# Combining weights of dilated attention broadcast one dilation at a time on GpSimd's queue, the next pair's q and k loaded earlier

## The chip, the cores and the metric

The kernel runs on one core of a Trainium2 chip. The core has five engines with a queue of instructions each: TensorE (PE, matrix products; PEld is its weight load), VectorE (DVE), ScalarE (ACT), GpSimd (POOL) and SyncE (SP, which only issues DMAs here). Each engine works through its own instructions in order; DMAs can be issued by SyncE, ScalarE and GpSimd. The metric is the device time of one execution in microseconds (us).

## The reference, cut to what matters

One decoder layer on 2048 positions of 1024 features. The input is projected; one branch is a Mamba-2 scan (chunked, with a convolution and a gate), the other is causal attention of 16 heads of 64 in a dilated window, computed for three dilations and then combined:

```python
o1, l1 = dilated_window_attention(q, k, v, slopes, 1)
o2, l2 = dilated_window_attention(q, k, v, slopes, 4)
o3, l3 = dilated_window_attention(q, k, v, slopes, 16)
wts = softmax(stack([l1, l2, l3]), axis=0)          # l: log of the sum of exponentials, per head and position
y_att = wts[0][..., None] * o1 + wts[1][..., None] * o2 + wts[2][..., None] * o3
y_att = rms_norm(y_att * silu(z_att), att_norm_g)
y_ssm = rms_norm(ssd(...) * silu(z_ssm), ssm_norm_g)
x = layer_norm(alpha * x + concat([y_att, y_ssm]) @ w_out, ln_g, ln_b)
```

Everything is float32. For each dilation a query sees itself and the 128 keys before it at that stride; the exponentials are not divided by their sum at once, but the sums enter the weights `wts`.

## The kernel before, in words

The kernel has three stages. The first, to about 1165 us, computes the projections, the convolution and the scan, and is not touched. It leaves in DRAM, per pair of heads, q and k (`d_q`, `d_k`, 128 x 2048), the gate (`d_za`), v in two row orders (`d_v`), and for the output projection the scan's rows (`d_us`) and the output weights (`d_wo`).

**Attention** (to about 1656 us) goes over 8 pairs of heads (`pr`). Two heads fill the 128 partitions. For each pair come the three dilations d = 0, 1, 2 (strides 16, 4, 1), for each of these four quarters `qd` of the query blocks, and for each quarter two halves: 24 steps, written (pr, d, qd, half). The step list is `todo` (L1234); the loop at L1239 writes at its turn i the scores of step i, the transposes of step i-2 and the values of step i-3. The order of the program inside this loop is what TensorE, VectorE, ScalarE and GpSimd execute (`manual_schedule`); only the order of SyncE's queue is left to the scheduler.

- `scores`: TensorE computes S = q·k for both heads. VectorE evicts it with the bias table `tb` added (L945); the same instruction leaves the row minimum of the scaled scores in a column of the statistics tile `st`. ScalarE takes the exponential and leaves the row sums in `st` (L951).
- `transposes`: TensorE transposes the exponentials, VectorE copies them to `PT`, `PC` (L968).
- `values`: TensorE multiplies with v and `vs` (v shifted by 64 rows); after the second half ScalarE copies the product N to `num[d]` (L1016 for d = 0, L1019 and L1022 for the others).
- `statistics` (L1025) transposes `st`, copies it to `sT`, and SyncE stores it to `d_st`: part 0 (d = 0 and 1) after step (1,3,1), part 1 (d = 2) after step (2,3,1), L1044.
- `gather` (L1050), right behind part 1, loads the pair's statistics back as `cm` (128 x 6 x 32: minimum and sum of three dilations, 128 x 32 positions). It is a DMA on GpSimd's queue, and waits for the stores to `d_st`.
- `weights` (L1053) makes the three combining weights per position from `cm`, nine small VectorE operations and an exponential on ScalarE, in two parts, after the values of steps (0,2,1) and (0,3,0) of the next pair. SyncE stores them to `d_wd` (L1068).
- `combine` (L1070), k = 0 to 5, all on GpSimd: k = 0, 1, 3 multiply `num[0]`, `num[1]`, `num[2]` by the weights of the dilation, which are broadcast from `d_wd` to all partitions of a tile `wb` by two DMAs of 512 KB on SyncE (L1081); k = 2 and 4 add; k = 5 multiplies by the gate, which SyncE loads into `wb` (L1096), and SyncE stores the result to `d_ua` (L1099). There are three buffers `wb` and six `num`.

Tables next to the loop hang other work behind the values of a step. `STEPS` (L1219) names for a step the part k of `combine` for the pair before, and a load: q and k of the next pair behind combine 0 and 1, at (1,0,0) and (1,1,0), v and vs for a dilation, all on GpSimd's queue (L862, L878, L880). `permute` (L904, L908) copies q into the order of a dilation on GpSimd. `LOADS` (L1222) does the same in the last pair for 1 MB tiles of `d_wo`, into buffers that attention no longer needs (`load_w`, L1116).

**The tail** (from about 1656 us) is the output projection: 16 blocks of 128 rows, each with two branches (`br` 1 is the scan, 0 attention) and two halves of the columns. `items` is the order of these products; a product (L1175 to L1177) uses a row `u` split into a rounded part on ScalarE and a rest on VectorE (`split`), fetched by `fetch_raw`; `squares` (L1143 to L1151) gives the root mean square; `add` puts the scaled product on the residual row `O`; `norm` is the layer norm. The first eight products are of the scan's rows, while pair 7 is still combined, on VectorE this time: its `weights` are written after item 1, its `combine` 0 to 2 after item 3 and 3 to 5 after item 4. The last one writes `u7` (L1092).

Of the kernel before, what the change touches and what calls it, by code (L numbers as in the profile page):

```python
# [9 lines left out]
F32 = mybir.dt.float32  # L10
# [18 lines left out]
def hybrid_layer(ctx, tc, xb, xc, w52, wv, wdt, convw, convb, dtb, alog, dskp, gcol, wout,  # L29
# [812 lines left out]
    with ExitStack() as c2:  # L842
# [137 lines left out]
        def values(A, d, qd, half, pts):  # L980
# [31 lines left out]
            if half == 1:  # L1012
                for i in range(2):
                    nm = A["N"][i][:, 0:256]
                    if d == 0:
                        nc.scalar.copy(f2(num[:, 4 * qd + 2 * i:4 * qd + 2 * i + 2, :]), nm)  # L1016
# [30 lines left out]
        def gather(A):  # L1047

            cm = A["cm"] = cm_.tile([128, 3, 2, 32], F32, name="cm")
            nc.gpsimd.dma_start(cm, dap(d_st[A["pr"]], 0, [[32, 128], [2 * S, 6], [1, 32]]))  # L1050

        def weights(A, part):

            m_, s_ = A["cm"][:, :, 0], A["cm"][:, :, 1]
            if part == 0:
# [3 lines left out]
                nc.vector.tensor_tensor(m_, mm[:, None, :].to_broadcast([128, 3, 32]), m_, op=OP.subtract)  # L1059
                nc.scalar.activation(m_, m_, AF.Exp)  # L1060
                return
            mm = A["mm"]
            nc.vector.tensor_tensor(s_, s_, m_, op=OP.mult)
# [3 lines left out]
            nc.vector.tensor_tensor(m_, m_, mm[:, None, :].to_broadcast([128, 3, 32]), op=OP.mult)
            nc.sync.dma_start(dap(d_wd[A["pr"]], 0, [[32, 128], [2 * S, 3], [1, 32]]), m_)  # L1068

        def combine(A, k):  # L1070
# [6 lines left out]
            if k in (0, 1, 3):  # L1077
                d = k - k // 2
                wb = A["wb"] = cm_.tile([128, NR, NJ], F32, name="wb", bufs=3)
                for h in range(2):  # L1080
                    nc.sync.dma_start(f2(wb[64 * h:64 * h + 64]),  # L1081
                                      dap(d_wd[pr], (d * 2 + h) * S, [[0, 64], [1, S]]))
# [11 lines left out]
            else:  # L1094
# [4 lines left out]
                nc.sync.dma_start(dap(d_ua, pr * 128, [[7 * 128, 128], [128 * 7 * 128, 16], [1, 128]]),  # L1099
# [24 lines left out]
        def fetch_raw(n, br, u=None):  # L1124
            u = raw[n, br] = (row() if u is None else u).rearrange("p (c t) -> p c t", t=128)
            queue = nc.gpsimd if (n, br) in ((3, 1), (0, 0), (1, 0)) else nc.sync
# [67 lines left out]
        def norm(n):  # L1194
# [10 lines left out]
            if n == 15:  # L1205
                for s in (slice(0, 512), slice(512, D)):
# [12 lines left out]
        STEPS = {(0, 0, 0): (None, "v", 0, 2), (0, 0, 1): (None, "vs", 0, 2), (1, 0, 0): (0, "q", 1),  # L1219
                 (1, 1, 0): (1, "k", 1), (1, 2, 0): (2, "v", 1, 0), (1, 3, 0): (3, None, 0), (2, 0, 0): (None, "v", 1, 1),  # L1220
# [8 lines left out]
        with tc.manual_schedule(engines={E.PE, E.DVE, E.Activation, E.Pool}):  # L1229
# [70 lines left out]
            for e in range(12, 16):  # L1300
                load_w(e, 1)
# [140 lines left out]
```

## Time and profile before

| | |
|---|---|
| time, median of 3 runs | 2046.55 us (2044.74 to 2047.88) |
| profiled execution: its time, its span | 2048.57 us, 2046.8 us |
| TensorE busy, weight loads | 1962.7 us (96%), 1598.1 us |
| VectorE, ScalarE, GpSimd busy | 1272.3, 1127.9, 1039.0 us |
| granted TensorE clock, mean | 0.986 |
| DMA | 447.72 MB, 219 GB/s over the span |

The rows shown below have these forms. A row of the timeline begins with the start in us and the duration; then come engine (SPq and POOLq are the DMA issues on these queues), line, operation, output<-input, the shapes, how many instructions stand together, and in brackets the idle time of the engine just before it with what ended it ("issue": nothing that the profile shows). A row of the windows has the stretch, its length, busy time and instructions of PE, PEld, DVE, ACT and POOL, the granted TensorE clock, the busy share of the DMA engines and GB/s. A row of the waits has engine, waiting operation, what it waits for, the sum in us, the number of waits, and the longest. The duration of a DMA row is that of its issue, not of its transfer. TensorE instructions are pipelined, so neighbouring rows overlap a little. Operations on GpSimd and VectorE that share a line are told apart by their tiles.

### The profile page before, as it was taken

The numbers are of one execution on the slowest core, as the hardware profiler recorded it, in microseconds if no ns is written. First come the engines' busy times: TensorE is split into PE (matmuls) and PEld (weight loads), VectorE is DVE, ScalarE is ACT, GpSimd is POOL, SyncE is SP. The second block draws the span as 40 slices with busy tenths as digits, with TensorE's granted clock in tenths as the row PEclk, the third lists the DMA queues.
The fourth block names the chain that finished last, engine by engine and source line by source line (L and its number), as shares of the span: only waits on it lengthen the run. The fifth ranks groups of instructions, "written<-read, shape, count | busy, mean of one in ns | idle before, by whom it ended". The sixth has DMA issues, their size and how long they took to land.

```text
span 2046.8 us, 42731 instructions
## 1 busy us (share of the span) xinstructions
PE 1962.7 (96%) x16024; PEld 1598.1 (78%) x16024; DVE 1272.3 (62%) x3181; ACT 1127.9 (55%) x3069; POOL 1039.0 (51%) x885
## 2 busy tenths in 40 slices
PE   7999999999999999999999999998989998999998
PEld 6788888888888888988888776666766676888886
DVE  7455464677775666644544387877777766665553
ACT  4455442466555766456566488887878851222220
POOL 3466613656655667155555424668766562432222
PEclk8999999999999999999999999999999999999999
DMA  7578695466778776987888856777787789323220
GB/s 272 164 265 288 221 331 188 133 195 194 242 252 304 252 250 252 328 264 256 277 270 268 271 179 184 215 218 236 223 235 226 217 262 314 115 97 103 87 69 31
DMA packets 232078, 447.72 MB, mean 219 GB/s; under 512 B 39520, under 2 KB 113760, under 8 KB 220864
## 3 DMA queue, kind: packets, MB, share of 16 engines
q1 hardware_dynamic: 139920, 190.02, 29.4%
q0 software_dynamic: 44000, 161.12, 23.3%
q10 hardware_dynamic: 47952, 93.87, 14.6%
q8 instruction: 126, 2.06, 0.4%
q14 instruction: 80, 0.66, 0.1%
HBM read 301.91 MB, written 151.39 MB: 221 GB/s over the span
## 4 chain that ended last, share of the span: by engine, by line
PE 81%; DMA 6%; DVE 5%; ACT 3%; issue 2%; POOL 1%; SPq 1%; ACTq 0%; POOLq 0%; DVEq 0%
PE pp L251 13%; PE pp L255 13%; PE pp L253 13%; PE N L992 5%; PE S L939 4%; PE S L1175 4%; PE S L1177 4%; PE S L1176 3%; PE pp L300 3%; PE T L966 3%; ACT P L951 2%; PE ss L300 2%; PE T L1175 2%; PE T L1176 2%; PE T L1177 2%
## 5 line engine op out<-in xcount | busy, mean ns | idle before, releaser
L208 POOL TENSOR_TENSOR w<-wr,w 128x512 fp32r<-128x512 f32 x224 | 294.0, 1324 | 225.2 <-ACT w L207 193.3
L951 ACT ACTIVATE P<-P,st 128x192 f32<-128x192 f32 (+1 forms) x768 | 322.1, 421 | 72.5 <-DVE st L945 67.7
L243 ACT COPY ev<-pp 128x512 f32<-128x512 f32 x200 | 116.5, 586 | 318.4 <-PE pp L255 283.5
L945 DVE CUSTOM_DVE_ANT_0 P<-S,tb 128x192 f32<-128x192 f32 (+1 forms) x768 | 206.5, 325 | 101.3 <-PE S L939 74.2
L263 DVE TENSOR_TENSOR ev<-pp,ev 128x512 f32<-128x512 f32 x152 | 101.2, 686 | 148.2 <-PE pp L255 100.9
L1083 POOL TENSOR_TENSOR wb<-num,wb 128x2048 f32<-128x2048 f32 x21 | 95.4, 4543 | 119.5 <-DMA wb<-d_wd 67.7
L207 ACT CAST w<-wr 128x512 fp32r<-128x512 f32 x224 | 133.6, 619 | 19.9 <-issue 7.4
L951 ACT ACTIVATION_READ_ACCUMULATOR P<-P,st 128x1 f32 x768 | 144.3, 188 | 0.0
L992 PE MATMUL N<-PT,v 128*64 128x64 f32 (+1 forms) x1536 | 125.3, 260 | 11.6 <-ACT num L1016 9.2
L968 DVE COPY PT<-T 128x512 f32<-128x512 f32 x192 | 131.7, 686 | 3.9 <-PE T L966 3.8
L966 PE MATMUL T<-ident,P 128*128 128x128 f32 x768 | 128.1, 290 | 0.3 <-DVE PT L968 0.2
L939 PE MATMUL S<-k,ex 64*64 64x192 f32 (+1 forms) x2048 | 113.0, 329 | 10.6 <-issue 10.5
L966 PEld LDWEIGHTS T<-ident,P 128*128 128x128 f32 x768 | 82.0, 142 | 47.3 <-issue 22.1
L992 PEld LDWEIGHTS N<-PT,v 128*64 128x64 f32 x1536 | 78.3, 137 | 49.2 <-issue 19.0
L202 DVE TENSOR_TENSOR wr<-wr 128x512 f32<-128x512 f32 x128 | 109.4, 854 | 8.8 <-DMA wr<-w 4.1
L454 DVE SCALAR_TENSOR_TENSOR ss<-U,cw,ss 128x512 f32<-128x512 f32 x144 | 106.0, 752 | 4.8 <-ACT ss L450 2.5
L1151 DVE TENSOR_REDUCE tb<-P 128x128 f32<-128x1024 f32 x30 | 60.0, 2000 | 44.9 <-ACT P L1148 22.5
L1213 POOL TENSOR_TENSOR k<-k,wb 128x1024 f32<-128x1024 f32 x8 | 25.8, 3225 | 120.4 <-DVE k L1212 120.4
L939 PEld LDWEIGHTS S<-k,ex 64*64 64x64 f32 x2048 | 68.1, 137 | 23.9 <-issue 17.8
L580 ACT ACTIVATE mt<-csb,cs 128x128 f32<-128x128 f32 x256 | 78.5, 392 | 1.2 <-DMA csb<-d_cs 1.2
L589 DVE TENSOR_TENSOR mt<-mt,ss 128x1024 f32<-128x1024 f32 x32 | 39.0, 1220 | 53.0 <-ACT mt L585 52.6
L251 PE MATMUL pp<-TB11h,w 128*128 128x512 f32 x176 | 69.6, 395 | 0.0
(480 smaller groups left out, 6045.0 us busy)
## 6 DMA issues: line engine op xcount, KB each, us to landing
wr<-w ACTq DMA_DIRECT2D x164, 256.0 KB
d_wc<-w SPq DMA_DIRECT2D x48, 512.0 KB
w<-d_wc POOLq DMA_DIRECT2D x48, 512.0 KB, 5.9
wb<-d_wd SPq DMA_DIRECT2D x48, 512.0 KB
d_wo<-wot POOLq DMA_DIRECT2D x32, 512.0 KB, 4.3
csb<-d_cs ACTq DMA_DIRECT2D x32, 512.0 KB
v<-d_v POOLq DMA_DIRECT2D x16, 1024.0 KB, 6.7
vs<-d_v POOLq DMA_DIRECT2D x16, 960.0 KB, 8.5
```

The lines of the kernel that those rows point to most:

```text
L207: nc.scalar.copy(h, r)
L208: nc.gpsimd.tensor_tensor(l, r, h.bitcast(F32), op=OP.subtract)
L251: nc.tensor.matmul(ps, w[:, 0, k], th[:, k], start=start and k == 0, stop=False, skip_group_check=not start)
L253: nc.tensor.matmul(ps, w[:, 0, k], tl[:, k], start=False, stop=False, skip_group_check=not start)
L255: nc.tensor.matmul(ps, w[:, 1, k], th[:, k], start=False, stop=(k == 3), skip_group_check=not start)
L939: nc.tensor.matmul(o, A["q"][d][64 * h:64 * h + 64, blk, 64 * a:64 * a + 64], kv, start=True, stop=True)
L945: nc.vector.tensor_tensor_reduce(P[:, h, cs], sp[h][:, cs], t, -0.125, 3.0e38, OP.add, OP.min, accum_out=stat(A, 0, d, h, blk))
L951: nc.scalar.activation(p, p, AF.Exp, bias=stat(A, 0, d, h, blk), scale=-1.0, accum_out=stat(A, 1, d, h, blk))
L966: nc.tensor.transpose(tp[:, h, i], P[:, h, 256 * i:256 * i + 128], ident)
L968: nc.vector.tensor_copy(pt, tp)
L992: nc.tensor.matmul(o, l, r, start=start, stop=True, skip_group_check=True)
L1175: nc.tensor.matmul(ps, uh[:, e, :], wh, start=(e == 0), stop=False)
```

## The change

The change leaves the arithmetic as it is, and moves where and when parts of it run.

- `broadcast` is a function of its own, on GpSimd's queue (SyncE's for pair 7). Dilation 0 is broadcast behind the weights at (0,3,0); the broadcast for k = 1 stands at the start of combine 0, the one for k = 3 at the start of combine 1.
- `weights` has three parts, at (0,2,0), (0,2,1) and (0,3,0). The two minima and the reciprocal stay on VectorE, the exponential on ScalarE; the subtraction, two multiplications and two additions run on GpSimd (VectorE for pair 7). The store to `d_wd` goes to GpSimd's queue (SyncE's for pair 7).
- q and k of the next pair are loaded at (0,1,0) and (0,2,0).
- Of the copies of N for d = 0 every second one runs on VectorE.
- In the last pair `gather` is on SyncE, v and vs for d = 2 are loaded at (1,0,0) and (1,0,1), the tiles of `d_wo` come at other steps, the second column halves of tiles 12 to 15 and the residual rows 0 and 1 before the end of attention.
- In the tail the weights of pair 7 are written ahead of the first item, combine 0 to 2 with the loads behind it after item 2, and 3 to 5 after item 3; residual rows 2 and 3 go to ScalarE's queue; the store of `u` of pair 6 goes to GpSimd's queue.

```diff
@@ values @@
                     if d == 0:
-                        nc.scalar.copy(f2(num[:, 4 * qd + 2 * i:4 * qd + 2 * i + 2, :]), nm)
+                        copy = nc.vector.tensor_copy if i else nc.scalar.copy
+                        copy(f2(num[:, 4 * qd + 2 * i:4 * qd + 2 * i + 2, :]), nm)
@@ gather, weights @@
-            nc.gpsimd.dma_start(cm, dap(d_st[A["pr"]], 0, [[32, 128], [2 * S, 6], [1, 32]]))
+            (nc.sync if A["pr"] == 7 else nc.gpsimd).dma_start(cm, dap(d_st[A["pr"]], 0, [[32, 128], [2 * S, 6], [1, 32]]))
...
+            last = A["pr"] == 7
+            eng = nc.vector if last else nc.gpsimd
             if part == 0:
                 mm = A["mm"] = cm_.tile([128, 32], F32, name="mm")
                 nc.vector.tensor_tensor(mm, m_[:, 0], m_[:, 1], op=OP.min)
                 nc.vector.tensor_tensor(mm, mm, m_[:, 2], op=OP.min)
-                nc.vector.tensor_tensor(m_, mm[:, None, :].to_broadcast([128, 3, 32]), m_, op=OP.subtract)
+                eng.tensor_tensor(m_, mm[:, None, :].to_broadcast([128, 3, 32]), m_, op=OP.subtract)
+            mm = A["mm"]
+            if part == 1:
                 nc.scalar.activation(m_, m_, AF.Exp)
...
+                eng.tensor_tensor(s_, s_, m_, op=OP.mult)
+                eng.tensor_tensor(mm, s_[:, 0], s_[:, 1], op=OP.add)
+                eng.tensor_tensor(mm, mm, s_[:, 2], op=OP.add)
+            if part == 2:
+                nc.vector.reciprocal(mm, mm)
+                eng.tensor_tensor(m_, m_, mm[:, None, :].to_broadcast([128, 3, 32]), op=OP.mult)
+                (nc.sync if last else nc.gpsimd).dma_start(dap(d_wd[A["pr"]], 0, [[32, 128], [2 * S, 3], [1, 32]]), m_)
+
+        def broadcast(A, k):
+            d = k - k // 2
+            wb = A["w", k] = cm_.tile([128, NR, NJ], F32, name="wb", bufs=3)
+            for h in range(2):
+                (nc.sync if A["pr"] == 7 else nc.gpsimd).dma_start(
+                    f2(wb[64 * h:64 * h + 64]), dap(d_wd[A["pr"]], (d * 2 + h) * S, [[0, 64], [1, S]]))
@@ combine @@
             if k in (0, 1, 3):
                 d = k - k // 2
-                wb = A["wb"] = cm_.tile([128, NR, NJ], F32, name="wb", bufs=3)
-                for h in range(2):
-                    nc.sync.dma_start(f2(wb[64 * h:64 * h + 64]),
-                                      dap(d_wd[pr], (d * 2 + h) * S, [[0, 64], [1, S]]))
+                if last:
+                    broadcast(A, k)
+                elif k < 3:
+                    broadcast(A, 2 * k + 1)
+                wb = A["wb"] = A.pop(("w", k))
                 eng.tensor_tensor(wb, A["num"][d], wb, op=OP.mult)
...
-                nc.sync.dma_start(dap(d_ua, pr * 128, [[7 * 128, 128], [128 * 7 * 128, 16], [1, 128]]),
+                (nc.gpsimd if pr == 6 else nc.sync).dma_start(dap(d_ua, pr * 128, [[7 * 128, 128], [128 * 7 * 128, 16], [1, 128]]),
@@ residual @@
-            (nc.gpsimd if n < 4 else nc.sync).dma_start(o, xc[n * 128:(n + 1) * 128, :])
+            (nc.gpsimd if n < 2 else nc.scalar if n < 4 else nc.sync).dma_start(o, xc[n * 128:(n + 1) * 128, :])
@@ the loop of attention @@
-        STEPS = {(0, 0, 0): (None, "v", 0, 2), (0, 0, 1): (None, "vs", 0, 2), (1, 0, 0): (0, "q", 1),
-                 (1, 1, 0): (1, "k", 1), (1, 2, 0): (2, "v", 1, 0), ...
+        STEPS = {(0, 0, 0): (None, "v", 0, 2), (0, 0, 1): (None, "vs", 0, 2), (0, 1, 0): (None, "q", 1), (0, 2, 0): (None, "k", 1),
+                 (1, 0, 0): (0, None, 0), (1, 1, 0): (1, None, 0), (1, 2, 0): (2, "v", 1, 0), ...
-        LOADS = {(0, 0, 1): ((8, None, "k_0"), (9, None, "q_0")), (1, 0, 0): ((10, None, "ex"),),
-                 (1, 1, 0): ((11, None, "vs"),), (1, 2, 0): ((12, 0, "q_1"),), (1, 3, 0): ((13, 0, "v"),),
-                 (2, 1, 0): ((14, 0, "v"), (15, 0, "vs"))}
+        LOADS = {(0, 0, 0): ((8, None, "k_0"),), (1, 0, 1): ((9, None, "q_0"),), (1, 1, 0): ((10, None, "ex"),),
+                 (1, 2, 0): ((11, None, "vs"),), (1, 2, 1): ((12, 0, "q_1"),), (1, 3, 0): ((13, 0, "v"),),
+                 (2, 0, 0): ((14, 0, "v"), (15, 0, "vs")), (2, 1, 0): ((12, 1, None), (13, 1, None)),
+                 (2, 1, 1): ((14, 1, None), (15, 1, None))}
-                    if pr and at in ((0, 2, 1), (0, 3, 0)):
-                        weights(pairs[pr - 1], qd - 2)
+                    if pr and at in ((0, 2, 0), (0, 2, 1), (0, 3, 0)):
+                        weights(pairs[pr - 1], 2 * qd + half - 4)
+                    if pr and at == (0, 3, 0):
+                        broadcast(pairs[pr - 1], 0)
@@ the tail @@
-            for e in range(12, 16):
-                load_w(e, 1)
...
+            for n in range(3):
+                weights(A, n)
...
-                if i == 1:
-                    weights(A, 0)
-                    weights(A, 1)
                 if i == 2:
...
+                    for j in range(3):
+                        combine(A, j)
+                    load_w(0, 0, "num")
+                    fetch_raw(3, 1)
+                    residual(2)
+                    residual(3)
```

GpSimd's instructions behind one gather in the middle of attention (the number at the end of a DRAM tile's name is the pair's copy; v, vs, q, k are the loads). Before:

```order
L1050 DMA cm<-d_st_116 128x6x32
L880 DMA v<-d_v_84 128x16x128
L880 DMA vs<-d_v_84 128x15x128
L1083 TENSOR_TENSOR wb<-num,wb 128x2048
L862 DMA q<-d_q_66 128x2048
L1083 TENSOR_TENSOR wb<-num,wb 128x2048
L862 DMA k<-d_k_74 128x2048
L1087 TENSOR_TENSOR wb<-wb 128x2048
```

And in the changed kernel, to the first broadcast:

```order
L1051 DMA cm<-d_st_116 128x6x32
L880 DMA v<-d_v_84 128x16x128
L880 DMA vs<-d_v_84 128x15x128
L862 DMA q<-d_q_66 128x2048
L1062 TENSOR_TENSOR cm<-mm,cm 128x3x32
L862 DMA k<-d_k_74 128x2048
L1066 TENSOR_TENSOR cm<-cm 128x3x32
L1067 TENSOR_TENSOR mm<-cm 128x32
L1068 TENSOR_TENSOR mm<-mm,cm 128x32
L1071 TENSOR_TENSOR cm<-cm,mm 128x3x32
L1072 DMA d_wd_124<-cm 128x3x32
L1079 DMA wb<-d_wd_124 64x2048 x4
```

The loads of q and k and the weights' operations stand between vs and the store of the weights, which was on SyncE's queue; the broadcasts (four issues, two dilations) stand right behind that store.

VectorE at the end of attention and the first items of the tail, from the squares of the first row of the scan. Before:

```order
L1151 TENSOR_REDUCE tb_19809<-ex 128x128
L1186 RECIPROCAL st<-st 128x1
L1143 TENSOR_TENSOR ex<-P,ex 128x1024
L1151 TENSOR_REDUCE tb_19845<-P 128x128
L1186 RECIPROCAL st<-st 128x1
L1057 TENSOR_TENSOR mm<-cm 128x32
```

And in the changed kernel:

```order
L1164 TENSOR_REDUCE tb_19811<-ex 128x128
L1060 TENSOR_TENSOR mm<-cm 128x32
L1061 TENSOR_TENSOR mm<-mm,cm 128x32
L1062 TENSOR_TENSOR cm<-mm,cm 128x3x32
L1066 TENSOR_TENSOR cm<-cm 128x3x32
L1067 TENSOR_TENSOR mm<-cm 128x32
L1068 TENSOR_TENSOR mm<-mm,cm 128x32
L1070 RECIPROCAL mm<-mm 128x32
L1071 TENSOR_TENSOR cm<-cm,mm 128x3x32
L1199 RECIPROCAL st<-st 128x1
L1156 TENSOR_TENSOR ex<-P,ex 128x1024
```

The weights of pair 7 moved ahead of the split of the third row (the rest `ex<-P,ex`), which stood ahead of them.

More of the change, by code (lines that the diff above doesn't have):

```diff
@@ L1125, in fetch_raw @@
             u = raw[n, br] = (row() if u is None else u).rearrange("p (c t) -> p c t", t=128)
-            queue = nc.gpsimd if (n, br) in ((3, 1), (0, 0), (1, 0)) else nc.sync
+            queue = nc.gpsimd if (n, br) in ((0, 0), (1, 0)) else nc.sync
             if br:
@@ L1275, in hybrid_layer @@
                         k, x, nx, *dd = STEPS[at]
+                        if pr == 7 and k is None and d == 0:
+                            x = None
                         if pr and k is not None:
@@ L1282, in hybrid_layer @@
                                 load_x(pairs[pr + nx], x)
+                    if pr == 7 and at in ((1, 0, 0), (1, 0, 1)):
+                        load_v(pairs[7], ("v", "vs")[half], 2)
                     if at == (2, 2, 0) and pr < 7:
@@ L1288, in hybrid_layer @@
                         load_w(e, hf, name)
+                    if at == (2, 3, 0):
+                        os_.append(big("k_1", F32))
+                        for n in range(2):
+                            residual(n)
                     if at == (2, 0, 0):
@@ L1297, in hybrid_layer @@
             small = stp.tile([128, 192], F32, name="st")
-            os_ += [big("k_1", F32), X]
+            os_.append(X)
             free.append(big("ex"))
-            for e in range(12, 16):
-                load_w(e, 1)
             fetch_raw(2, 1)
@@ L1305, in hybrid_layer @@
             squares(1, 1)
-            for n in range(2):
-                residual(n)
+            for n in range(3):
+                weights(A, n)
             ops = [(n, 1) for n in range(4)] + [(n, 0) for n in range(4)]
@@ L1336, in hybrid_layer @@
                     squares(*ops[j])
-                    for m in (3,) if j == 2 else (j + 2,) if 4 < j < 30 else ():
+                    for m in (j + 2,) if 4 < j < 30 else ():
                         fetch_raw(*ops[m])
@@ L1342, in hybrid_layer @@
                 if i == 3:
-                    for j in range(3):
-                        combine(A, j)
-                    load_w(0, 0, "num")
-                    residual(2)
-                    residual(3)
                     fetch_raw(0, 0)
-                if i == 4:
+                    for j in range(2, 4):
+                        scaled(j)
                     for j in range(3, 6):
                         combine(A, j)
+                        if j < 5:
+                            add(*adds.pop(0))
+                if i == 4:
                     for e, name in enumerate(("num", "vs", "v", "wb", "num", "wb", "num")):
@@ L1362, in hybrid_layer @@
                     split(0, 0)
-                    for j in range(2, 4):
-                        scaled(j)
                     while adds:
```

10 lines of the change are left out of this document (1 added, 9 removed).

## The prediction

> **What bounds the kernel now.** I read the stretches first, then the waits of each engine inside the attention stage, then one pair of heads in the timeline. Four stretches: projections and scan, attention, the first products of the output projection, the rest.
>
> ```profile
> 0.00:1165.00 1165.00, 1139.93 (x6181) 966.53 (x6182) 682.13 (x1008) 633.10 (x1172) 624.95 (x594) 0.99 0.74 249
> 1165.00:1640.00 475.00, 438.34 (x7900) 321.40 (x7898) 362.08 (x1847) 386.41 (x1716) 285.05 (x222) 0.97 0.74 218
> 1640.00:1730.00 90.00, 76.69 (x595) 60.21 (x594) 60.09 (x97) 35.24 (x77) 43.94 (x41) 0.94 0.95 296
> 1730.00:2047.00 317.00, 307.74 (x1354) 249.93 (x1353) 168.03 (x231) 73.16 (x105) 85.10 (x30) 0.99 0.26 88
> ```
>
> The change touches the second and third stretch. There TensorE (first busy number) is idle 36.7 and 13.3 us; GpSimd (last) is busy only 60% of attention. It would be easy to conclude that TensorE's waits set the pace. The timeline of one pair says something else. GpSimd's queue, from one gather of softmax statistics (cm<-d_st) to the next:
>
> ```profile
> 1484.23 0.87 POOL L1050 DMA_DIRECT2D cm<-d_st  x1 [3.22 <-DVE st L945]
> 1485.10 1.15 POOL L880 DMA_DIRECT2D v<-d_v  x1
> 1486.24 1.19 POOL L880 DMA_DIRECT2D vs<-d_v  x1
> 1502.60 4.50 POOL L1083 TENSOR_TENSOR wb<-num,wb 128x2048 f32<-128x2048 f32 x1 [15.17 <-DMA wb<-d_wd]
> 1507.04 0.60 POOL L862 DMA_DIRECT2D q<-d_q  x1
> 1508.65 4.53 POOL L1083 TENSOR_TENSOR wb<-num,wb 128x2048 f32<-128x2048 f32 x1 [1.01 <-DMA wb<-d_wd]
> 1513.14 0.60 POOL L862 DMA_DIRECT2D k<-d_k  x1
> 1513.77 4.56 POOL L1087 TENSOR_TENSOR wb<-wb 128x2048 f32<-128x2048 f32 x1
> ...
> 1532.39 4.55 POOL L1098 TENSOR_TENSOR wb<-wb 128x2048 f32<-128x2048 f32 x1
> 1536.88 2.79 POOL L904 COPY ex<-q 128x256 f32<-128x256 f32 x8
> 1539.62 2.27 POOL L908 COPY ex<-q 128x512 f32<-128x512 f32 x4
> 1545.33 0.87 POOL L1050 DMA_DIRECT2D cm<-d_st  x1 [3.44 <-DVE st L945]
> ```
>
> SyncE's queue in the same pair, and the two places where this work meets the other engines:
>
> ```profile
> 1490.48 0.38 SPq L1068 DMA_DIRECT2D d_wd<-cm  x1
> 1495.20 3.69 SPq L1081 DMA_DIRECT2D wb<-d_wd  x6
> 1536.97 0.37 SPq L1099 DMA_DIRECT2D d_ua<-wb  x1
> 1537.46 4.36 SPq L1044 DMA_DIRECT2D d_st<-sT  x4
> ...
> 1537.18 0.26 ACT L1035 COPY sT<-T 64x128 f32<-64x128 f32 x1
> 1487.01 0.19 DVE L1057 TENSOR_TENSOR mm<-cm 128x32 f32<-128x32 f32 x1 [0.73 <-DMA cm<-d_st]
> 1489.08 0.25 DVE L1063 TENSOR_TENSOR cm<-cm 128x96 f32<-128x96 f32 x1
> ```
>
> These rows close a loop. Call the gather's issue G. The weights go to DRAM and the broadcasts are issued at G + 10.97 (leg a); the first combination starts 7.40 later (leg b); 34.34 later, at 1536.94, the gated product is done (leg c). Only then may SyncE store it (1536.97), and the pair's last statistics stand behind that store on the same queue (1537.46), though their copy sT was ready at 1537.44; they land, and the next gather goes out at 1545.33, 8.39 after the product (leg d). Sum 61.1. VectorE takes its work in order, so its minimum on cm (1487.01, after 0.73 idle) holds back the score evictions behind it, and with them TensorE. Over all pairs:
>
> ```profile
> 1239.57 0.84 POOL L1050 DMA_DIRECT2D cm<-d_st  x1 [16.82 <-DMA d_st<-sT]
> 1606.24 0.87 POOL L1050 DMA_DIRECT2D cm<-d_st  x1 [3.30 <-DVE PT L968]
> DVE mm L1057 <- DMA cm<-d_st: 2.1, 4, 0.7
> ```
>
> Six loops take 366.67, 61.1 each, and VectorE waits for cm in four of eight pairs, never over 0.7: loop and TensorE are level now. Whatever lengthens the loop lengthens the kernel, six times; what only shortens TensorE's side gains nothing, unless the loop shortens too.
>
> **The change, part by part.** *Stalls that it is aimed at.* In this pair TensorE lost
>
> ```profile
> 1492.94 0.71 PE L992 MATMUL N<-PT,v 128*64 128x128 f32 x8 [1.67 <-ACT num L1016]
> 1507.18 0.92 PE L939 MATMUL S<-k,ex 64*64 64x192 f32 x8 [3.56 <-issue]
> 1500.00:1520.00 20.00, 16.25 (x305) 12.33 (x305) 11.71 (x56) 12.40 (x55) 16.37 (x8) 0.83 0.95 244
> ```
>
> 1.67 behind VectorE's weights, 3.56 while the six broadcasts ran, and about 3.4 of clock (0.83 over 20 us): some 8.6 of 61. Moving five of nine small operations off VectorE and half of the first dilation's copies of num off ScalarE may take most of the 1.67 away. But TensorE being level with the loop, these 8.6 become slack, not time. So edits here count 0, with the loop as cover; without that cover they would be worth up to 8 us a pair.
>
> *Leg a.* Before, only v and vs (2 MB) are on the way when the weights are written. Now q and k of the next pair (2 MB more) are issued right behind them and ahead of the weights' store, on the same queue; the first two broadcasts stand behind that store. The last pair of the old kernel already shows this load, for it fetches two 1 MB weight tiles at that place:
>
> ```profile
> 1609.44 0.60 POOL L1116 DMA_DIRECT2D k<-d_wo  x1
> 1610.02 0.57 POOL L1116 DMA_DIRECT2D q<-d_wo  x1
> 1629.57 4.51 POOL L1083 TENSOR_TENSOR wb<-num,wb 128x2048 f32<-128x2048 f32 x1 [18.98 <-ACT num L1019]
> ...
> 1613.09 0.38 SPq L1068 DMA_DIRECT2D d_wd<-cm  x1
> 1622.03 3.68 SPq L1081 DMA_DIRECT2D wb<-d_wd  x6
> ```
>
> The store took 8.94 to land instead of 4.72, and the broadcasts went out at G + 15.79 instead of 10.97, although the store had a queue of its own. Behind q and k on their queue I add 0.3 for its own landing: 16.1. The arithmetic hides under this: from cm's landing at G + 2.8, three steps of about 2 us (1487.01 to 1489.08 is one) and six short GpSimd operations (the nearest GpSimd row, a copy of 256 elements, is 0.35 each: 2.79 for 8) end by about G + 9. Bounds of the leg: 11.8 (weights done at 9, landing as fast as cm, 2.8) and 17.5 (1.5 more for a store that starts only after k).
>
> *Leg b.* No broadcast stands on GpSimd's queue in this trace. SyncE's row says 7.4 (7.54 in the last pair); GpSimd's k, the same 1 MB, lands in
>
> ```profile
> k<-d_k POOLq DMA_DIRECT2D x8, 1024.0 KB, 6.2
> ```
>
> I take 7.4, since source and destination are the broadcast's; low bound 6.2. The Trainium skill (DMA: Bandwidth & Descriptors, "Issuing engines are not separate DMA queues") says that the issuing engine saves issue time only and that all run on the same DMA engines; by it this leg stays too, and the trace agrees as far as store and loads on two queues above did delay each other.
>
> *Leg c.* q's and k's issues leave it (0.60 each), the third broadcast's two issues come in (0.6 each) where 1.01 of waiting stood: 33.7, between 33.0 and 34.3. *Leg d.* Unchanged, 8.4; in some pairs a table load (0.4 to issue) now stands between store and statistics: 8.2 to 9.3.
>
> Loop: 16.1 + 7.4 + 33.7 + 8.4 = 65.6, against 61.1: 4.5 more in each of six pairs, **+27**. Bounds: 11.8 + 6.2 + 33.0 + 8.2 = 59.2 and 17.5 + 7.9 + 34.3 + 9.3 = 69.0 (b at most half a microsecond above SyncE's).
>
> *One step sooner.* VectorE's minimum now comes one step (about 2 us) earlier in the pair. With the loop in front it makes no difference to the period; in the last pair about 2 us more work lie behind the gather, less some 1.4 of small operations: +0.6.
>
> *The tail.* Before:
>
> ```profile
> 1663.79 0.50 PE L1175 MATMUL S<-v,num 128*128 128x512 f32 x1 [3.30 <-DMA v<-d_wo]
> 1713.71 0.79 PE L1175 MATMUL S<-num 128*128 128x512 f32 x1 [6.27 <-DVE ex L1192]
> 1673.91 0.17 DVE L1057 TENSOR_TENSOR mm<-cm 128x32 f32<-128x32 f32 x1
> 1676.56 0.26 DVE L1067 TENSOR_TENSOR cm<-cm,mm 128x96 f32<-128x96 f32 x1
> 1707.98 2.50 DVE L1092 TENSOR_TENSOR PT<-wb,num 128x512 f32<-128x512 f32 x4
> ```
>
> The weight loads are issued a pair's third sooner: -3.3. The last gather moves to SyncE, free of GpSimd's product; I put the last combination (1707.98, 52 after attention's end at 1656.0) some 10 sooner, so most of the 6.27 goes: -4.7. Against that, the last weights (2.9 from 1673.91 to 1676.82, after a gather some 9 us behind attention's end) now stand on VectorE ahead of the split of the third activation row, which TensorE needs 11 us after attention's end and gets after about 14: +3. Clock after the vanished stalls: -2. Sum **-7**, between -12 and 0.
>
> Total 27 + 0.6 - 7 = +20.6. Against the profiled execution (span 2046.8, its time 2048.57) that is a span of 2067.4. The median of the runs, 2046.55, is 2.0 under the profiled execution, so the forecast for the median is 2046.55 + 20.6 = **2067**.
>
> **Rivals.** *Not slower: the store of the weights slips past q and k.* Then leg a is about 11.8, where the arithmetic ends, and b may shrink to 6.2; the loop is 11.8 + 6.2 + 33.7 + 8.4 = 60.1, six times -1.0, and with the tail 2046.55 - 6 - 7 = 2033; with b as before 61.3, 2041. It decides as soon as leg a falls under some 12.4. For it: the store is 48 KB of 4 MB. Against: in the last pair it stood on another queue than k and q and still landed only with them.
>
> *Loop a little longer, hidden by the tail.* Loop about 62 (a 13, b 7): +6 - 7 gives 2046, no change. For it: broadcasts come two at a time, so that less is queued; against: the first must still wait for the store.
>
> *TensorE takes over the loop.* Waiting for cm, TensorE idles some 7 us in a pair, and its clock falls; with two stalls of 3.56 under the spaced broadcasts and a further 3.4 of clock its own way from cm to sT, 50.4 now, would reach 57 and more, past the product at G + 57.2. Loop 68, +41 - 7: 2081. The Trainium skill (TensorE: Matmul & The Clock Gate, "Part 1: The HAM clock gate") says that idleness halves the clock and about 3.4 us of activity restore it; the trace agrees with 0.83 in the window above.
>
> **How the numbers follow.** Forecast, loop 64 to 67.5 and tail -12 to 0: 0.60, 2052 to 2084. TensorE takes over: 0.12, 2076 to 2088. Hidden by the tail: 0.08, 2043 to 2050. Slips past: 0.20, 2030 to 2042, since no store of this size on the loads' own queue stands in this trace. I call a difference within 0.2% (4.1 us) none, since a measurement of this kernel tells no less: faster 0.20, same 0.08, slower 0.72. The range that leaves out no more than two in ten is 2038 to 2084; the forecast's own is 2052 to 2084.
>
> **What would show it.** Right: the wait of VectorE's minimum for cm grows from 2.1 us in all to 25 or more, and TensorE idles in the third quarter of the first dilation of each pair; G to G is 65 to 66; the first broadcast is issued at G + 15 to 17, the first combination at G + 23 to 25. TensorE's issue waits beside the broadcasts may stay, without costing anything. In the tail a wait of some 3 us appears before the third row's product, and the 3.30 for v is gone. Wrong: G to G of 61 or less, or a store of the weights that lands within 4 us; then the TensorE stalls were the bound and the kernel is faster.

## The result, and the profile after

The changed kernel takes 2073.56 us (median of 4 runs, 2072.39 to 2078.32), the kernel before 2047.22 (4 runs): ratio 1.0139, 95% interval 1.0122 to 1.0157. The forecast was slower, 2067 in a range of 2038 to 2084.

The profiled execution of the changed kernel took 2078.32 us and is the longest of the four; its first gather already stands 4.55 us later than before (1244.12 against 1239.57), in a stage that the change does not touch. The three other runs took 2072.4 to 2073.7. So of the 29.75 us between the two profiled executions, 25.2 lie behind the first gather, and these are the ones to explain.

The first and the last gather on GpSimd's queue of the changed kernel (timeline), and two lines of the waits (engine, operation, what it waited for, sum, number, longest):

```profile
1244.12 0.84 POOL L1051 DMA_DIRECT2D cm<-d_st  x1 [16.79 <-DMA d_st<-sT]
1636.30 0.87 POOL L1051 DMA_DIRECT2D cm<-d_st  x1 [1.61 <-DMA d_st<-sT]
...
DVE mm L1060 <- DMA cm<-d_st: 46.9, 7, 8.5
PE N L992 <- DVE st L945: 40.1, 6, 8.0
```

Six loops take 392.18, 65.36 each, against 61.11: 25.5 us, which is the whole difference. VectorE's minimum waits 46.9 us for cm (2.1 before), and TensorE 40.1 behind VectorE. The windows over these six loops, the kernel before first:

```profile
1239.57:1606.24 366.67, 336.22 (x6210) 248.69 (x6211) 283.35 (x1445) 299.60 (x1337) 248.38 (x175) 0.97 0.78 223
```

```profile
1244.12:1636.30 392.18, 343.31 (x6264) 254.13 (x6264) 286.73 (x1448) 294.66 (x1321) 282.51 (x247) 0.94 0.71 209
```

TensorE does the same work and is idle 48.9 us instead of 30.5; its granted clock falls from 0.97 to 0.94, and the DMA engines carry less per time. Only GpSimd got busier by much, 282.5 us instead of 248.4, with the issues that moved to it (24 us) and five of the eight (not nine) small operations of the weights (10 us), and it still idles 110 us. The loop got longer. One turn of it on GpSimd's queue:

```profile
1507.09 0.87 POOL L1051 DMA_DIRECT2D cm<-d_st  x1 [3.03 <-DMA tb<-tabs]
1511.23 0.58 POOL L862 DMA_DIRECT2D k<-d_k  x1
1514.22 0.39 POOL L1071 TENSOR_TENSOR cm<-cm,mm 128x96 f32<-128x96 f32 x1 [0.47 <-DVE mm L1070]
1514.91 0.84 POOL L1072 DMA_DIRECT2D d_wd<-cm  x1 [0.29 <-POOL cm L1071]
1523.71 2.07 POOL L1079 DMA_DIRECT2D wb<-d_wd  x4 [7.96 <-DMA d_wd<-cm]
1531.60 4.54 POOL L1096 TENSOR_TENSOR wb<-num,wb 128x2048 f32<-128x2048 f32 x1 [5.83 <-DMA wb<-d_wd]
1560.44 4.56 POOL L1111 TENSOR_TENSOR wb<-wb 128x2048 f32<-128x2048 f32 x1
1571.60 0.87 POOL L1051 DMA_DIRECT2D cm<-d_st  x1 [1.65 <-DMA d_st<-sT]
```

The weights are done at G + 7.5 (1514.61) and stored at G + 7.8. The store lands 8.80 later, behind v, vs, q and k. The broadcasts go out at G + 16.62. How the loop closes again, SyncE's queue and the last copy of the statistics on ScalarE:

```profile
1565.03 0.37 SPq L1112 DMA_DIRECT2D d_ua<-wb  x1
1565.49 4.34 SPq L1045 DMA_DIRECT2D d_st<-sT  x4
...
1559.93 0.26 ACT L1036 COPY sT<-T 64x128 f32<-64x128 f32 x1
```

sT is ready at 1560.19, 4.8 before the product's store lets the statistics go. Over the six loops it is ready at G + 50.7 to 54.2, the product's store goes at G + 57.7 to 58.9: TensorE now has slack in every pair, 3.9 us or more.

| leg, mean of six loops (us) | before | forecast | after |
|---|---|---|---|
| a: gather to first broadcast's issue | 11.33 | 16.1 | 16.60 |
| b: to the first combination | 7.61 | 7.4 | 8.07 |
| c: to the issue of the product's store | 34.18 | 33.7 | 33.53 |
| d: to the next gather | 8.00 | 8.4 | 7.16 |
| loop | 61.11 | 65.6 | 65.36 |

(The legs are differences of the start times of such rows. Legs c and d are cut at the store's issue here, a few hundredths behind the product's end.)

Behind the last gather, the last pair and the tail, TensorE's rows with a wait:

```profile
1641.77 1.12 PE L992 MATMUL N<-PT,v 128*64 128x128 f32 x8 [4.80 <-DVE st L945]
1660.94 0.37 PE L992 MATMUL N<-PC,v 64*64 64x64 f32 x2 [2.91 <-issue]
1682.63 0.21 PE L992 MATMUL N<-PC,v 64*64 64x64 f32 x1 [2.06 <-issue]
...
1708.30 0.80 PE L1188 MATMUL S<-k,ex 128*128 128x512 f32 x1 [5.59 <-ACT ex L1154]
```

From the last gather to the end of the last copy sT the changed kernel takes 54.75 us (1636.30 to 1691.05), the one before 50.66 (1606.24 to 1656.90): +4.1. From there to the end of the span it takes 385.4 instead of 389.9: -4.5. Together nothing.

### The profile page after: what moved, and what is told of

Its sections match the earlier page's. It is cut to its first block, busy times and chain, and to the rows that moved or that the text cites. A ratio compares the mean times of both kernels' runs of the same rounds, so it can differ in the third digit from the quotient of the medians.

```text
span 2076.5 us, 42753 instructions
## 1 busy us (share of the span) xinstructions
PE 1971.3 (95%) x16024; PEld 1604.0 (77%) x16024; DVE 1271.6 (61%) x3178; ACT 1116.8 (54%) x3035; POOL 1078.0 (52%) x965
## 4 chain that ended last, share of the span: by engine, by line
PE 83%; DMA 5%; DVE 5%; ACT 3%; issue 2%; SPq 1%; POOL 0%; ACTq 0%; DVEq 0%; POOLq 0%
PE pp L251 13%; PE pp L255 13%; PE pp L253 13%; PE N L992 7%; PE S L939 5%; PE T L966 4%; PE pp L300 3%; PE S L1188 3%; PE S L1190 3%; PE S L1189 3%; PE ss L300 2%; ACT P L951 2%; PE T L1188 2%; PE T L1190 2%; PE T L1189 2%
## 5 line engine op out<-in xcount | busy, mean ns | idle before, releaser
L208 POOL TENSOR_TENSOR w<-wr,w 128x512 fp32r<-128x512 f32 x224 | 294.6, 1327 | 225.1 <-ACT w L207 191.0
L992 PE MATMUL N<-PT,v 128*64 128x64 f32 (+1 forms) x1536 | 128.2, 265 | 41.8 <-DVE st L945 40.1
L1164 DVE TENSOR_REDUCE tb<-P 128x128 f32<-128x1024 f32 x30 | 60.2, 2007 | 45.4 <-ACT P L1161 23.0
L589 DVE TENSOR_TENSOR mt<-mt,ss 128x1024 f32<-128x1024 f32 x32 | 39.0, 1219 | 54.9 <-ACT mt L585 54.5
L232 POOL TENSOR_TENSOR w<-wr,w 128x512 fp32r<-128x512 f32 x36 | 46.3, 1286 | 45.3 <-ACT w L231 45.2
```

Of the source, the lines that this page charges most:

```text
L208: nc.gpsimd.tensor_tensor(l, r, h.bitcast(F32), op=OP.subtract)
L992: nc.tensor.matmul(o, l, r, start=start, stop=True, skip_group_check=True)
```

## The experiments

The theory under test: the loop sets the pace, and a small transfer (gather, store of the weights, statistics) lands only with the large loads issued shortly ahead of it, on whichever queue. The rivals: the earlier minimum on VectorE is the price; the order on GpSimd's queue is the price; a queue of its own protects the store; the tie between product and gather alone sets the pace.

**q and k back** behind combine 0 and 1, in the changed kernel:

```diff
-... (0, 1, 0): (None, "q", 1), (0, 2, 0): (None, "k", 1), (1, 0, 0): (0, None, 0), (1, 1, 0): (1, None, 0),
+... (1, 0, 0): (0, "q", 1), (1, 1, 0): (1, "k", 1),
```

> The changed kernel with the loads of q and k put back behind combine 0 and 1. Loop theory (the store of the weights lands only behind the loads issued ahead of it, and that leg lies on the loop from gather to gather): leg a falls from 16.6 to about 12.3 (weights done at G + 7.8, landing 4.2 to 4.7 as with v and vs alone), b 7.5, c 34.3 (two issues back in), d 7.2 to 8.2: loop 61.3 to 62.3 against 65.4, time 2073.6 - 6 x 3.6 = 2052 (2047 to 2056). Rival 1 (the minimum written one step earlier makes VectorE and TensorE wait, q and k do not matter): over 2064. Rival 2 (the broadcasts on GpSimd's queue are slow): over 2064.

Measured: 2048.11 us, 1.0024 of before (1.0012 to 1.0036). The loop is 61.69. GpSimd's queue (timeline):

```profile
1482.74 0.87 POOL L1051 DMA_DIRECT2D cm<-d_st  x1 [3.50 <-DMA tb<-tabs]
1490.61 0.81 POOL L1072 DMA_DIRECT2D d_wd<-cm  x1 [0.29 <-POOL cm L1071]
1494.36 2.09 POOL L1079 DMA_DIRECT2D wb<-d_wd  x4 [2.94 <-DMA d_wd<-cm]
```

The store lands after 3.75 instead of 8.80, leg a is 11.62. With all else of the change in place, moving two loads takes 25 of its 26 us away: neither the earlier minimum nor the broadcasts' queue is the price. What is left of the change gains nothing, too.

**Only q and k early**, in the kernel before; the store stays on SyncE's queue, the loads are on GpSimd's:

```diff
-(1, 0, 0): (0, "q", 1), (1, 1, 0): (1, "k", 1),
+(0, 1, 0): (None, "q", 1), (0, 2, 0): (None, "k", 1), (1, 0, 0): (0, None, 0), (1, 1, 0): (1, None, 0),
```

> The kernel before with nothing but the loads of q and k moved to (0,1,0) and (0,2,0); the weights' store and the broadcasts stay on SyncE. Loop theory: leg a 15.3 to 15.8 as in the last pair of the kernel before, b 7.5, c 33.2, d 8.1: loop about 64.3 against 61.1, time 2047.2 + 19 = 2066 (2060 to 2071). Rival (what delays the store is that it stands behind q and k on one queue; on a queue of its own it slips past): leg a about 11.5, loop 60 to 61.5, time 2043 to 2050.

Measured: 2072.46 us (2065.68 to 2073.49), 1.0133 of before (1.0114 to 1.0151); loop 64.61 in the profiled run, which is the fastest. SyncE's queue there:

```profile
1498.98 0.38 SPq L1068 DMA_DIRECT2D d_wd<-cm  x1
1508.37 3.76 SPq L1081 DMA_DIRECT2D wb<-d_wd  x6
```

9.39 to land, on a queue on which nothing else was issued for 7 us. The two loads alone make the old kernel as slow as the changed one. The time lies just above the 2060 to 2071 expected; the loop is 0.3 longer than forecast.

**Store and broadcasts back on SyncE**, in the changed kernel:

```diff
-(nc.sync if last else nc.gpsimd).dma_start(dap(d_wd[A["pr"]], ...), m_)
+nc.sync.dma_start(dap(d_wd[A["pr"]], ...), m_)
-(nc.sync if A["pr"] == 7 else nc.gpsimd).dma_start(f2(wb[64 * h:64 * h + 64]), ...)
+nc.sync.dma_start(f2(wb[64 * h:64 * h + 64]), ...)
```

> The changed kernel with the store of the weights and all broadcasts back on SyncE, q and k still early. Loop theory: the store lands with q and k all the same, leg a 15 to 16, b 7.5, c 32.5 to 33.5, d 7.2: loop 63.5 to 64.5, time 2073.6 - 8 = 2066 (2060 to 2071). Rival (the order on GpSimd's queue is the cause): leg a under 12.5, time 2044 to 2054.

Measured: 2067.89 us, 1.0117 (1.0102 to 1.0132).

```profile
1507.52 0.38 SPq L1072 DMA_DIRECT2D d_wd<-cm  x1
1516.06 3.68 SPq L1079 DMA_DIRECT2D wb<-d_wd  x6
```

8.54 to land: the queue is not the cause. The time fits the expectation, but its sum does not: the loop is 65.38, not 64. Of the 5.7 us between the medians the trace places 3.6 in the last pair and the tail (from the last gather of the loop to the end 436.6 us against 440.2); the first gather also stands 5.2 us sooner, in a stage that the edit does not touch.

**The minimum back** behind the values of (0,2,1), in the changed kernel:

```diff
-if pr and at in ((0, 2, 0), (0, 2, 1), (0, 3, 0)):
-    weights(pairs[pr - 1], 2 * qd + half - 4)
+if pr and at in ((0, 2, 1), (0, 3, 0)):
+    for n in ((0,), (1, 2))[qd - 2]:
+        weights(pairs[pr - 1], n)
```

> The changed kernel with the minimum and the subtraction back behind the values of (0,2,1), and the other two parts of the weights together at (0,3,0). Loop theory: the arithmetic lies in the shadow of q and k, TensorE's wait for cm is slack of the loop: period still 65 to 66, only the last pair gains some 2: time 2071 (2067 to 2075); VectorE's wait for cm falls from 46.9 by about 2 in each of seven pairs, and TensorE waits as long elsewhere. Rival (VectorE's wait for cm is itself the price): 7 x 2.1 less, 2059 (2056 to 2063).

Measured: 2071.82 us, 1.0133 (1.0118 to 1.0149); loop 65.14.

```profile
DVE mm L1060 <- DMA cm<-d_st: 33.0, 7, 6.0
```

VectorE waits 13.9 us less, 2.0 in each of seven pairs, and the time does not follow. A long wait in the list is a price only if the waiting engine leads; here it is slack showing itself.

**The product's store on GpSimd's queue**, in the kernel before (the test of "level"):

```diff
-nc.sync.dma_start(dap(d_ua, pr * 128, ...), ...)
+nc.gpsimd.dma_start(dap(d_ua, pr * 128, ...), ...)
```

> The kernel before with one edit: the gated product is stored from GpSimd's queue, so that SyncE's stores of the last statistics no longer stand behind it. If loop and TensorE are level, as the prediction said (sT is ready within 1.2 us of the product in every pair), nothing is won: leg d 7.5 to 8.3, loop 60.5 to 61.5, time within 4 us of before. If TensorE has slack there, the loop falls by 1 to 2: 6 to 12 us faster.

Measured: 2048.53 us, 1.0012 (0.9998 to 1.0027): no difference; loop 61.25. The statistics are issued at sT now, yet the gather goes out no sooner: behind the product stand the issue of its 1 MB store (1.2) and the permutes (5.1) on GpSimd, and another 1.3 to 3.1 of waiting for the statistics to land. They land 2.2 to 6.2 after their last issue, while the 1 MB goes out beside them on the other queue. So this run fits "level" but does not test it alone: it moves the store without taking it out of the way. The last run below does.

**The loop cut**: gather on SyncE, product's store on GpSimd, in the changed kernel; and **the same with q and k back**:

```diff
-(nc.sync if A["pr"] == 7 else nc.gpsimd).dma_start(cm, dap(d_st[A["pr"]], ...))
+nc.sync.dma_start(cm, dap(d_st[A["pr"]], ...))
-(nc.gpsimd if pr == 6 else nc.sync).dma_start(dap(d_ua, ...), ...)
+nc.gpsimd.dma_start(dap(d_ua, ...), ...)
```

> The changed kernel with the loop cut: the gather on SyncE for all pairs and the gated product stored from GpSimd's queue, so that neither gather nor statistics wait for the product. q and k stay early. Then GpSimd's own chain is next: from cm 4.5 to the weights' store, 8.3 landing, 7.9 broadcast, 33.4 combination, 1.2 issue of the store, 5.1 permutes, 3.4 issues and one operation = 63.8 against a loop of 65.4: 2073.6 - 10 = 2064 (2058 to 2070), and VectorE waits for GpSimd's weights instead of for cm. Rival (the tie of gather and product alone sets the period, and TensorE's 53 from gather to sT plus 5 follow when it is cut): loop 58, 2030.

Measured: 2064.43 us, 1.0099 (1.0062 to 1.0137), as GpSimd's chain would have it; the five runs spread from 2059.47 to 2079.25, and the trace is of one at 2061.79. Two loops of 58.5 and 58.3, then 63.8, 63.5, 63.6 and 65.8: as soon as GpSimd's backlog is built up, its own chain (63.8 forecast) is the pace.

> The same cut, and q and k back behind combine 0 and 1. GpSimd's chain: 4.5 + 4.3 + 7.5 + 34.4 + 1.2 + 5.1 + 2.8 = 59.8; TensorE's own way 58 to 60. Loop theory: about 60, 2048 - 10 = 2038 (2032 to 2044), faster than the kernel before. Rival (TensorE's stalls beside the broadcasts grow with the overlap): no faster than 2046.

Measured: 2071.87 us, 1.012 (1.0098 to 1.0142): the expectation fell, the loop is 63.64. The first loop takes 55.2, the later ones 64 to 66. GpSimd's queue and, below, SyncE's and VectorE's rows at one gather:

```profile
1492.72 1.16 POOL L880 DMA_DIRECT2D v<-d_v  x1
1493.87 1.19 POOL L880 DMA_DIRECT2D vs<-d_v  x1
1503.38 0.38 POOL L1062 TENSOR_TENSOR cm<-mm,cm 128x96 f32<-128x96 f32 x1 [8.32 <-DVE mm L1061]
```

```profile
1494.99 0.38 SPq L1051 DMA_DIRECT2D cm<-d_st  x1
...
1502.88 0.19 DVE L1060 TENSOR_TENSOR mm<-cm 128x32 f32<-128x32 f32 x1 [5.33 <-DMA cm<-d_st]
```

GpSimd no longer waits with v and vs until the gather is out. Their 2 MB go first, and the gather takes 7.9 to land instead of 2.8. The theory under test had this in it; I had applied it to the store of the weights only.

**The same with the permute moved and the tail's weights back** (the permute for the third dilation behind the first broadcast; `weights` of the last pair after the second item):

```diff
-if (d, qd, half) == (0, 0, 0):
-    permute(pairs[pr], 2)
+if at == (0, 3, 0):
+    permute(pairs[pr], 2)
...
+if i == 1:
+    for n in range(3):
+        weights(A, n)
```

> As the run before it, and two edits more: the permute of q for the third dilation stands behind the first broadcast (GpSimd waits there anyway), which takes 2.3 out of GpSimd's chain, and the weights of the last pair stand behind the second product of the tail again. If GpSimd's chain is the bound there: 57.5, and TensorE with its 58 decides: 6 x 1.8 less; the tail's wait of 5.4 for the third row's split goes: -5. Together 2022 (2014 to 2030). If TensorE is already the bound: only the tail, 2033.

Measured: 2077.07 us, 1.0142 (1.0105 to 1.018); loop 63.94, from 54.5 to 72.1. v and vs now come 2.3 sooner still, among the statistics' stores; SyncE's and GpSimd's queues in one of the long loops:

```profile
1550.22 3.25 SPq L1045 DMA_DIRECT2D d_st<-sT  x4
1562.68 0.38 SPq L1051 DMA_DIRECT2D cm<-d_st  x1
```

```profile
1551.36 1.15 POOL L880 DMA_DIRECT2D v<-d_v  x1
1552.50 1.21 POOL L880 DMA_DIRECT2D vs<-d_v  x1
```

From the last statistics' issue, at 1553.5, the gather behind them waits over 9 us.

**Only the tail's weights back**, in the changed kernel (the last three lines of the diff above, and the loop ahead of the items taken out):

> The changed kernel with one edit in the tail: the weights of the last pair are written behind the second product again (as before the change), so that VectorE and ScalarE split the third row ahead of waiting for cm. The loop is not touched. If that wait is what TensorE's 5.6 before the third row's product is made of: 2073.6 - 5 = 2068 (2064 to 2071), and no wait over 2 there. If the split is late for another reason (its row lands late): 2071 to 2075.

Measured: 2078.5 us, 1.0159 (1.0139 to 1.0178): not faster, the expectation was wrong. The wait of 5.59 is gone, and TensorE (above) and VectorE (below) wait elsewhere:

```profile
1732.44 0.80 PE L1190 MATMUL S<-k,num 128*128 128x512 f32 x1 [9.79 <-DVE num L1156]
...
1721.80 2.29 DVE L1096 TENSOR_TENSOR wb<-num,wb 128x2048 f32<-128x2048 f32 x1 [9.27 <-DMA wb<-d_wd]
```

The weights come later, so the broadcasts do, and VectorE waits for them ahead of the next row's split. The early weights of the change are worth some 4 us of this wait (9.79 against 5.59); the two ratios, 1.0159 and 1.0139, do not tell the kernels apart.

**All large loads behind the small transfers**, with the cut, the permute and the tail as two runs above (v and vs for the third dilation behind combine 0, q behind combine 1, k a step later):

```diff
-(0, 0, 0): (None, "v", 0, 2), (0, 0, 1): (None, "vs", 0, 2), (0, 1, 0): (None, "q", 1), (0, 2, 0): (None, "k", 1),
-(1, 0, 0): (0, None, 0), (1, 1, 0): (1, None, 0),
+(1, 0, 0): (0, None, 0), (1, 1, 0): (1, "q", 1), (1, 1, 1): (None, "k", 1),
...
-if pr == 7 and at in ((1, 0, 0), (1, 0, 1)):
-    load_v(pairs[7], ("v", "vs")[half], 2)
+if pr and at in ((1, 0, 0), (1, 0, 1)):
+    load_v(pairs[pr], ("v", "vs")[half], 2)
```

> The loop cut as in the two runs before, the tail's edit, the third dilation's permute behind the first broadcast, and in addition every large load put behind the small transfers: v and vs for the third dilation behind combine 0, q behind combine 1, k a step later. Theory (a small transfer lands only with the loads issued ahead of it, on whichever queue): gather lands 2.8 after its issue in every pair, the weights' store 2.5 to 3; GpSimd's chain 4.5 + 2.6 + 7.2 + 37 + 1.2 + 2.8 + 0.4 = 55.7, TensorE's own way 55 to 58.5 (the first loops of the runs with the cut were 54.5 to 58.5): loop 57 to 58.5, 2048 - 4 x 6 - 5 = 2019 (2010 to 2028). Rival (the loads now collide with the broadcasts, and legs b and c grow as much as a shrinks): 2035 to 2050.

Measured: 2053.02 us, 1.0033 (1.0016 to 1.005); loop 60.98. The store of the weights lands in 2.4 to 2.8 in every pair, as the theory says, but the forecast of 2019 fell. Legs b and c are 7.42 and 37.50, near the forecast (7.2 and 37), so the rival that they grow explains 0.7 us of the loop's excess. TensorE's waits:

```profile
PE N L992 <- DMA vs<-d_v: 11.5, 7, 3.7
PE S L1190 <- DVE num L1156: 10.5, 1, 10.5
```

The loads are late themselves now (11.5), the tail's wait is the one of the run before, and the gather is not always clear: where the product's 1 MB store went out 2 us ahead of it, the minimum came at G + 4.8 and 5.4, where 7.5 or more ahead, at G + 2.2 and 2.5.

**The same without the cut and the permute's move**:

> The same places for the loads and the tail's edit, but without the cut: gather on GpSimd behind the product, the product's store on SyncE, the permute in its old place. Legs: a 10.4, b 7.2, c 36.5 (the issues of v and vs now stand in it), d 7: loop 61.1; 2048.1 - 6 x 0.6 - 5 = 2039 (2033 to 2045). If the cut is what matters beside the loads, this run stays some 15 to 25 above the cut one; if the loads' place alone matters, both are equal.

Measured: 2066.79 us, 1.0103 (1.0071 to 1.0134); loop 64.74 instead of 61.1, so the forecast of 2039 fell. a is 10.74, near the expected 10.4, but c is 38.1 on average instead of 36.5, with the issues of v and vs in it, and d 8.5 instead of 7. The distance to the cut run is 14 us, just under the 15 to 25 expected if cut and place both matter.

**The kernel before with leg d alone shortened**: the product is stored from ScalarE's queue some 17 to 23 us later, in the middle of the next turn (for pair 6 at once), away from gather, weights' store and last statistics; the permute and the table as described:

```diff
-                nc.sync.dma_start(dap(d_ua, pr * 128, ...), u.rearrange("p (n t) -> p n t", t=128))
+                A["u"] = u
+                if pr == 6:
+                    nc.sync.dma_start(dap(d_ua, pr * 128, ...), u.rearrange("p (n t) -> p n t", t=128))
...
-                    if (d, qd, half) == (0, 0, 0):
-                        permute(pairs[pr], 2)
-                    if pr and at == (0, 3, 0):
+                    if at == (0, 3, 0):
+                        permute(pairs[pr], 2)
+                    if pr and at == (0, 0, 0):
                         load_tab(pairs[pr], 2)
+                    if pr > 1 and at == (1, 0, 1):
+                        nc.scalar.dma_start(dap(d_ua, (pr - 2) * 128, ...), pairs[pr - 2]["u"]...)
```

> The kernel before with its loop shortened at leg d alone, and loads, weights and tail as they were: the gated product of a pair is stored from ScalarE's queue one pair later, behind the values of (1,0,1), so that the 1 MB does not stand ahead of the last statistics; the permute of q for the third dilation moves from ahead of the gather to (0,3,0), where GpSimd waits for broadcasts, with the table for that dilation loaded at (0,0,0). Theory (the loop sets the pace, and small transfers land behind the large ones ahead of them): the statistics are issued at sT, G + 52.8 to 54.7, land by G + 57 to 58, GpSimd is free at product + 2.8 = G + 56.2: d falls from 8.1 to 4.5, loop 57.5 to 59 where TensorE allows it (minimum at G + 2.8, 50.4 to sT, 4.5 to the gather: 57.7); 6 x 2.5 less, 2045.5 - 15 = 2031 (2024 to 2039). If TensorE's stalls beside the broadcasts are level with the loop and grow with it: sT comes later in the pair, loop 60 to 61, no change (2041 to 2047).

Measured: 2037.68 us (2033.23 to 2043.66), 0.9953 of before (0.9937 to 0.9969): faster than both kernels. GpSimd's and SyncE's rows of one turn:

```profile
1535.79 2.78 POOL L904 COPY ex<-q 128x256 f32<-128x256 f32 x8
1539.79 0.87 POOL L1050 DMA_DIRECT2D cm<-d_st  x1 [1.21 <-DVE st L945]
```

```profile
1533.93 2.10 SPq L1044 DMA_DIRECT2D d_st<-sT  x4
```

The statistics are issued before the product ends, and GpSimd has finished the permute 1.2 ahead of the gather. VectorE no longer waits for cm in any pair (the list of its waits has no such line), and the last four loops are 59.4 to 60.2: TensorE's own way is the bound there, with the stalls that the change was aimed at still in it:

```profile
PE N L992 <- issue: 10.1, 7, 3.2
PE N L992 <- ACT num L1016: 8.8, 7, 1.6
```

The time is inside the 2024 to 2039 expected, but the loop of 57.5 to 59 was too low by that: it is 60.40 on average. The profiled run is the slowest of the six (4.9 us under the profiled run of before); where the other runs, 5 to 10 us faster, gain the rest is not shown by a trace.

## Why the prediction was right

**The bound.** "Loop and TensorE are level; whatever lengthens the loop lengthens the kernel, six times": the six loops make 25.5 us, and the whole time behind the first gather grew by 25.2. The level held to about 1 us a loop: before, sT is ready between 0.7 us ahead of the product's store and 1.2 behind it, and with the last run's shorter leg d TensorE's own way brings the last four loops only from 60.6 to 61.6 down to 59.4 to 60.2. "What only shortens TensorE's side gains nothing" held too. Of TensorE's waits in attention, these two in the kernel before,

```profile
PE S L939 <- issue: 12.0, 6, 3.6
PE N L992 <- ACT num L1016: 9.2, 7, 1.7
```

the second is gone from the changed kernel's list and the first is down to 1.6, and nothing of it came out of the time: the wait for cm took its place. With q and k back the 9.2 are gone as well, and the rest of the change still gained nothing.

**Leg a** was forecast at 16.1 and is 16.60: the arithmetic hides (7.8, forecast 9), and the store lands 8.4 later on average. (Its upper bound, 16.1 + 1.5, is 17.6, not 17.5.) The rival in which the store slips past q and k is refuted by three kernels, on the loads' queue and off it. **Leg b** was forecast 0.7 under the measurement, **c** 0.2 above, **d** 1.2 above. Of d's 1.2, 0.4 come from the turn it was read from (8.39, where the mean of six is 8.00), the rest because the statistics land sooner (1.8 after the last issue in the turn shown, 3.5 before); b and d lie outside the bounds given, b 6.2 to 7.9 and d 8.2 to 9.3. That the statistics land sooner because less is on its way at that time (DMA share 0.71 against 0.78) is argued, not shown. The errors cancel: 65.6 forecast, 65.36 measured, +27 forecast, +25.5 measured. Leg a came out for the reason given; that the sum of the four fits to 0.2 is luck.

**One step sooner** was the term that was mis-sized: +0.6 forecast, +4.1 measured for the last pair. The forecast counted VectorE's work in that pair, but not that TensorE's wait for cm, which the next turn hides in six pairs, is hidden by nothing in the last: 4.80 of waiting, two issue stalls of 4.97 together, and 10.2 us at half clock behind them, against 1.00, 2.96 and 3.4 before. Putting the minimum back took 1.05 off the time from that gather to the last one (62.89 to 61.84), so the step itself is only a part.

**The tail** was forecast at -7 (-12 to 0) and gave -4.5. The wait of 3.30 for v and the one of 6.27 went, as forecast; the new wait was put at 3 and is 5.59, because the last cm lands 5.5 after its issue, behind 2 MB of `d_wo` issued 2.6 to 4.8 us ahead of it on GpSimd's queue.

**TensorE takes over** (0.12) did not come: its clock did fall, but its own way from VectorE's minimum to sT is 47.3 to 51.5 (47.7 to 50.9 before), not 57, with most of the stalls above out of it.

The sum was +20.6 on the profiled execution; behind the first gather it is 25.2, and the medians differ by 26.3. The 4.6 too few are the last pair (3.5) and the tail (2.5), less the loop (1.5).

## What to carry to other kernels

Look for the loop that a small transfer closes (statistics out, gathered, weights out, broadcast), add up its legs from one turn, and ask of every moved load whether it now goes out ahead of one of these transfers. A level engine's stalls are worth nothing until the loop is shorter; when it is, the same stalls are the next bound. To protect a small transfer, move the large one in time: another queue did not do it here.

## What was not expected of the hardware

How long the store of the weights (48 KB) takes from its issue to the broadcast behind it depends on the bytes issued shortly ahead, and hardly on the queue (means over six pairs; "ahead" is from the issue of the last large load named):

| ahead of it | queue of the store | us |
|---|---|---|
| nothing large, or v, vs (2 MB) 6.3 us or more ahead (five kernels) | SyncE or GpSimd | 2.49 to 2.64 |
| v, vs, 4.2 to 5.4 us ahead (8.2 in the first pair, which took 1.69) | SyncE, kernel before | 4.15 |
| v, vs, 5.8 to 6.3 us ahead (7.9 in the first pair, which took 2.42) | GpSimd, q and k back | 3.33 |
| v, vs, q, k (4 MB), 3.7 to 4.3 us ahead | GpSimd, changed kernel | 8.43 |
| the same, 2.4 to 4.1 us ahead (6.4 in one first pair) | SyncE | 8.31 and 8.86 |

The records of single packets in the traces show where the store waits. In the turn shown with only q and k early, the store was issued on SyncE's queue (q1) at 1498.98, the loads on GpSimd's (q0). None of the store's packets starts before 1502.75. Between 1502.7 and 1507.9 these ran (queue, packets, MB, share of 16 engines):

```profile
q0 software_dynamic: 246, 1.75, 79.6%
q1 hardware_dynamic: 400, 0.05, 6.2%
```

The store is 384 packets of 128 bytes on this queue (the other 16 have 4 bytes). They run over the same 5 us as the loads' packets of 8 KB, and the last ends at 1507.87, 0.09 us behind the last of q and k. In the changed kernel, on the loads' own queue, the same store is 16 packets of 3072 bytes; in the turn shown the last of them ends 0.14 us behind the last packet of 8 KB. The Trainium skill (DMA: Bandwidth & Descriptors, "Queues, rings and completion order") says that each DMA engine takes turns between the queues it has work for and changes at packet boundaries. The trace agrees in so far as the packets of both queues run side by side, and the store ends with the loads all the same. That it takes so long because 384 pieces need many turns is argued from these counts, not shown. What holds the first packet back by 3.77 us (0.89 in the last run, for the store at 1488.42), and whether a store of fewer, larger packets on a queue of its own would pass the loads, no run here shows. The same page ("Issuing engines are not separate DMA queues") says that transfers of all engines run on the same 16 DMA engines and that issuing from another saves issue time only; with that the runs agree.
